# A two-layer decoder trunk on one core: weight buffers from a list, three lags, a third decay buffer and a new order of units in its DeltaNet layer

## The chip, the cores and the metric

The kernel runs on one core of one Trainium2 chip. The metric is the device time of the whole program in microseconds (us), the median of several runs. The core has five engines that run side by side, each through its own list of instructions in a fixed order: TensorE (PE in the profile; its weight loads are PEld), VectorE (DVE), ScalarE (ACT), GpSimd (POOL) and SyncE (SP), which issues most of the DMAs. An instruction that waits holds up all that stands behind it on its engine.

## The reference

528 positions (16 learned meta tokens and 512 of the input) of width 1024 pass two layers; each is a mixer (forgetting attention in layer 0, gated DeltaNet in layer 1) and a feed-forward block with a causal convolution, each with a norm before and after. The change lies in the DeltaNet layer:

```python
def gated_deltanet(h, w_in, conv_w, a_log, dt_bias, o_gain, w_out):   # H=8 heads of 128
    proj = hp @ w_in
    qkv, og, b_logit, a_logit = split(proj)
    qkv = silu(causal_dwconv(qkv, conv_w))
    q, k = l2norm(q) * Dh ** -0.5, l2norm(k)
    beta, g = sigmoid(b_logit), -exp(a_log) * softplus(a_logit + dt_bias)
    gc = cumsum(g)                                    # in each chunk
    dec = exp(where(incl, gc_i - gc_j, -inf))
    A = where(strict, kk * dec * beta, 0)
    sol = triangular_solve(A + I, [kc * beta * exp(gc), vc * beta])
    W, U0 = split(sol)
    def step(S, xs):                                  # one chunk after the other
        U = U0_n - W_n @ S
        O = qd_n @ S + qk_n @ U
        S = gl_n * S + U^T @ kd_n
        return S, O
    O = rmsnorm(O, o_gain) * silu(og)
    return O @ w_out
h = h + rmsnorm(m, g_post);  f = conv_ffn(rmsnorm(h, g_ffn));  h = h + rmsnorm(f, g_ffn_post)
```

All is float32. The kernel uses chunks of 16 and four times 128 positions.

## The kernel before

Every projection is cut into units of 128 output columns (`_units`, L68). A unit's weights come by one DMA into a staging tile (two of them), ACT casts them to a high part (L288) and DVE or POOL computes the low part (L295); `dense` (L303) then makes three matmuls for each of the (mostly 8) tiles of the inner dimension. The positions lie in two halves of 272 and 256. `push` (L428) runs the first half of a unit at once and the second half after a lag of further units: 4 with six weight buffers (`wp`), 6 between `wide` and `narrow` (L1477), where two more buffers (`wx`) exist. `need` (L298) loads one unit ahead. `boundary` (L405) is the norm between blocks: a sum of squares on ACT and POOL, a power on POOL, transposes on PE, then eight tiles of DVE work; the next projection needs its outputs `xh` and `xl`, and the scale `r` when a result leaves PSUM.

The DeltaNet layer (`deltanet` L844, `dn_heads` L902) has 33 input units: one for the gates, then K, V, Q and H (the output gate) for four groups of two heads, in the order of `DNSEQ` (L42). The gates become decays, which go to DRAM and come back broadcast. For each group there is a chain: `decays` (L1051) fills a decay buffer (two, taken in turn by the groups), `gram_k` (L1079) and `gram_q` (L1118) make the products K·K and Q·K, `solve_meta` (L1153) inverts the block of the meta tokens, `solve` (L1192) takes the 32x32 diagonal blocks through DRAM to POOL for a substitution of 31 steps (L1214, L1215), takes the result back and joins the blocks by four rounds of matmuls (m1 to m4), and `scan` (L1277) runs one meta step and four chunk steps. `heads_out` (L1364) normalises a chunk's output and transposes it into O. `part` (L866) multiplies the first four heads' O by the output weights (eight units P of four inner tiles); after the layer has been flushed, `out_proj` (L453) adds the other four heads' half (eight more such units), and `boundary` follows.

The order of PE's work in this layer is planned while the program is built. `Flow` (L219) keeps a clock of its own: each dense tile adds to it, and after each tile the tasks whose planned time has come put their instructions there. The distances between the steps of a task are the constants at the top (`T_HOP`, `T_GATES`, `T_OUT` and so on, in us). Dense matmuls and scan matmuls keep exactly the order in which they were written (`tok`, L267). PSUM has eight banks; in this layer dense results have two (`d`), grams two (`e`), scan steps two (`f`), scan outputs one (`g`), and the transposes of `heads_out` and all products of the solves share one (`h`).

The group chain waits on these flags before the change:

```python
yield lambda: ("gates", half) in done and (g < 2 or ("scan", g - 2) in done) and (half or not g or ("meta", g - 1) in done)
...
if g:
    yield lambda: ("sub", g - 1) in done
yield from solve()
```

Of the kernel before, what the change touches and what calls it, by code (L numbers as in the profile page):

```python
# [29 lines left out]
T_HOP = 1.4  # L30
T_CONV = 7
T_SUMS = 4
T_GATES = 13
T_BLOCKS = 8
T_DMA = 3.5
T_STEP = 1.0
T_META = 2.0
T_BACK = 6
T_INV = 3
T_OUT = 3.5  # L40

DNSEQ = [(x[0], int(x[1])) for x in "K0 V0 Q0 K1 K2 Q1 V1 H0 Q2 K3 V2 H1 Q3 V3 H2 H3 P0 P1 P2 P3".split()]  # L42
# [25 lines left out]
def _units():  # L68
# [26 lines left out]
    for kind, g in DNSEQ:  # L95
        for hl in range(NG):
            if kind == "P":
                add("dn_w_out", 0, 0, 4, (NG * g + hl) * 128, 128)
                continue
            add("dn_w_in", 0, 0, 8, {"Q": 0, "K": 1024, "V": 2048, "H": 3072}[kind] + (NG * g + hl) * 128, 128)  # L100
    for m in range(8):
        add("dn_w_out", 0, 512, 4, m * 128, 128)
# [5 lines left out]
def trunk(ctx, tc, h0, wflat, params, out):  # L108
# [10 lines left out]
    wp = ctx.enter_context(tc.tile_pool(name="wp", bufs=6))  # L119
# [11 lines left out]
        "dn": {"ps": "d", "g": "e", "s": "f", "o": "g", "t": "h", "l": "h"},  # L131
# [87 lines left out]
    class Flow:  # L219
# [38 lines left out]
        def until(self, cond):  # L258
            assert not self.busy
            while not cond():  # L260
                t = min(self.ready(), key=lambda t: t["wake"])
# [13 lines left out]
    state = {"next": 0, "lag": LAG}  # L275

    def load(u):
        _, _, _, nk, _, M = units[u]
        n = nk * M
        pool = wp  # L280
        if "wx" in state and units[u][0] != "dn_w_in" and u % 4 == 3:
            pool = state["wx"]
        wl = pool.tile([P, n], F32R, name="wl", tag="wl")
        wh = pool.tile([P, n], F32R, name="wh", tag="wh")
        w32 = ws.tile([P, n], F32, name="w32", tag="w32")[:]
        with tc.high_priority(offset=0):
            nc.sync.dma_start(w32, wflat[int(offs[u]):int(offs[u + 1])].rearrange("(p f) -> p f", p=P))
            nc.scalar.copy(wh[:], w32)  # L288
# [14 lines left out]
    def dense(u, half, xh, xl, c0=0, c1=None):  # L303
# [4 lines left out]
        o = ps[:M, 0:c1 - c0]  # L308
        tot = 3 * nk
        i = 0  # L310
        for k in range(nk):
            a = slice(k * M, (k + 1) * M)
# [114 lines left out]

    def push(u, fn):  # L428
        need(u)
        while len(pending) >= state["lag"]:  # L430
            a, f = pending.pop(0)
            f(a, 1)
# [3 lines left out]
    def flush():  # L436
        while pending:
            a, f = pending.pop(0)
            f(a, 1)
# [404 lines left out]
    def deltanet(layer, post, pre, wcx):  # L844
# [5 lines left out]
        m = [None, None]  # L850

        def split(half, k0):
            c = CUT if half == 0 else 0
            n = HALF[half][1] if n_cut else HALF[half][1] - c
            x = take(half, "ohl", F32R, [P, 2, KT // 2, n])
# [6 lines left out]
        n_cut = []  # L862
# [3 lines left out]
        def part(u, half, mt):  # L866
            n = HALF[half][1] - (CUT if half == 0 else 0)
            if mt == 0:
                drop(*X[half][:2])
                m[half] = take(half, "m", shape=[P, KT, n])  # L870
                OHL[half] = split(half, 0)
            x = OHL[half]
            ps = dense(u, half, lambda k: x[:, 0, k, :], lambda k: x[:, 1, k, :], 0, n)
# [668 lines left out]
```

## Time and profile before

| | us |
|---|---|
| median of 3 runs (lowest, highest) | 1616.88 (1613.69, 1617.59) |
| the profiled execution's own time | 1616.02 |
| its span in the profile | 1614.3 |
| PE busy in the span | 1521.4 (94%) |
| PEld, DVE, ACT, POOL busy | 1489.7, 1140.3, 801.9, 458.2 |

PE's busy time is an upper bound of useful work: matmuls overlap in the pipeline, and the time counts at whichever clock the throttle grants. So the count of matmuls in a stretch, the granted clock (1.00 is 2.4 GHz, 0.5 is 1.2 GHz) and the gaps are to be read together.

### The profile page before, as it was taken

The numbers are of one execution on the slowest core, as the hardware profiler recorded it, in microseconds if no ns is written. First come the engines' busy times: TensorE is split into PE (matmuls) and PEld (weight loads), VectorE is DVE, ScalarE is ACT, GpSimd is POOL, SyncE is SP. The second block draws the span as 40 slices with busy tenths as digits, with TensorE's granted clock in tenths as the row PEclk, the third lists the DMA queues.
The fourth block names the chain that finished last, engine by engine and source line by source line (L and its number), as shares of the span: only waits on it lengthen the run. The fifth ranks groups of instructions, "written<-read, shape, count | busy, mean of one in ns | idle before, by whom it ended". The sixth has DMA issues, their size and how long they took to land.

```text
span 1614.3 us, 32996 instructions
## 1 busy us (share of the span) xinstructions
PE 1521.4 (94%) x12462; PEld 1489.7 (92%) x12462; DVE 1140.3 (71%) x2765; ACT 801.9 (50%) x1868; POOL 458.2 (28%) x951
## 2 busy tenths in 40 slices
PE   8999999999999999999779889899989999999996
PEld 6999999899999999999678879889978999999996
DVE  7888888949974675665878757675559864765764
ACT  6677777735543442343454355444555543433441
POOL 6434443125200010013544562633044100100112
PEclk9999999999999999999799789999998999999998
DMA  5332222422223222322233322221241323323321
GB/s 173 90 88 77 74 87 74 133 68 77 93 82 102 92 82 90 95 89 82 81 90 93 92 62 61 75 69 37 80 137 54 93 90 93 99 85 97 99 68 53
DMA packets 67680, 139.56 MB, mean 86 GB/s; under 512 B 22936, under 2 KB 35640, under 8 KB 67136
## 3 DMA queue, kind: packets, MB, share of 16 engines
q1 hardware_dynamic: 66896, 135.08, 28.2%
q8 instruction: 98, 1.61, 0.4%
q0 software_dynamic: 480, 2.15, 0.4%
q14 instruction: 62, 0.51, 0.1%
q10 hardware_dynamic: 144, 0.22, 0.0%
HBM read 132.06 MB, written 5.36 MB: 85 GB/s over the span
## 4 chain that ended last, share of the span: by engine, by line
PE 68%; DVE 11%; POOL 6%; DMA 5%; ACT 4%; issue 3%; SPq 2%; POOLq 0%; DVEq 0%; ACTq 0%
PE ps L315 62%; POOL RB L1215 3%; POOL PR L1214 3%; DVE h L415 1%; DVE bt L414 1%; DVE wl L295 1%; DMA w<-wflat 1%; PE av L701 1%; DVE cv L767 1%; DVE xl L381 1%; DMA AB<-dA 1%; PE pt L681 1%; DMA gcr<-gcd 1%; ACT wh L288 1%; DVE qr L580 1%
## 5 line engine op out<-in xcount | busy, mean ns | idle before, releaser
L315 PE MATMUL ps<-xh,wh 128*128 128x256 f32 (+4 forms) x2464 | 720.6, 294 | 26.6 <-DVE ub L751 19.1
L315 PE MATMUL ps<-xl,wh 128*128 128x256 f32 (+4 forms) x2464 | 713.4, 290 | 6.1 <-DVE xl L381 6.0
L315 PE MATMUL ps<-xh,wl 128*128 128x256 f32 (+4 forms) x2464 | 716.3, 291 | 0.0
L315 PEld LDWEIGHTS ps<-xh,wh 128*128 128x128 f32 (+1 forms) x2464 | 473.9, 193 | 31.2 <-DVE ub L751 11.9
L315 PEld LDWEIGHTS ps<-xl,wh 128*128 128x128 f32 (+1 forms) x2464 | 474.3, 193 | 10.2 <-DVE xl L381 8.1
L315 PEld LDWEIGHTS ps<-xh,wl 128*128 128x128 f32 (+1 forms) x2464 | 474.1, 193 | 0.9 <-DVE wl L295 0.3
L288 ACT CAST wh<-w 128x1024 fp32r<-128x1024 f32 (+3 forms) x226 | 224.9, 996 | 194.2 <-PE ps L315 166.2
L295 DVE TENSOR_TENSOR wl<-w,wh 128x1024 fp32r<-128x1024 f32 (+4 forms) x191 | 221.0, 1157 | 100.7 <-ACT wh L288 100.0
L767 DVE SCALAR_TENSOR_TENSOR cv<-ub,prm,cv 128x256 f32<-128x256 f32 (+2 forms) x494 | 244.0, 499 | 37.5 <-ACT cv L758 29.4
L315 PE MATMUL ps<-ah,wl 128*128 128x256 f32 (+2 forms) x704 | 199.8, 284 | 0.0
L315 PE MATMUL ps<-ah,wh 128*128 128x256 f32 (+2 forms) x704 | 199.6, 284 | 0.0
L315 PE MATMUL ps<-al,wh 128*128 128x256 f32 (+2 forms) x704 | 199.4, 284 | 0.0
L758 ACT ACTIVATE cv<-ub,prm 128x256 f32<-128x256 f32 (+2 forms) x224 | 113.5, 510 | 142.3 <-DVE ub L751 142.0
L751 DVE TENSOR_TENSOR ub<-ps,r 128x256 f32<-128x256 f32 (+2 forms) x224 | 95.3, 427 | 95.5 <-PE ps L315 94.7
L315 PEld LDWEIGHTS ps<-ah,wh 128*128 128x128 f32 x704 | 132.9, 189 | 0.0
L315 PEld LDWEIGHTS ps<-al,wh 128*128 128x128 f32 x704 | 132.7, 189 | 0.0
L315 PEld LDWEIGHTS ps<-ah,wl 128*128 128x128 f32 x704 | 132.6, 189 | 0.0
L356 POOL TENSOR_TENSOR ssq<-ssq,sq 128x256 f32<-128x256 f32 (+2 forms) x98 | 90.1, 922 | 148.4 <-ACT sq L355 146.9
L754 POOL COPY cy<-ub 128x2 f32<-128x2 f32 (+1 forms) x112 | 35.5, 319 | 294.1 <-DVE ub L751 293.3
L295 POOL TENSOR_TENSOR wl<-w,wh 128x512 fp32r<-128x512 f32 x70 | 94.5, 1370 | 72.1 <-ACT wh L288 56.7
L750 POOL COPY ub<-cy 128x2 f32<-128x2 f32 (+1 forms) x112 | 30.0, 268 | 208.2 <-DVE cv L767 172.7
L814 DVE TENSOR_TENSOR m<-m,ps 128x256 f32<-128x256 f32 (+2 forms) x64 | 27.2, 425 | 42.6 <-PE ps L315 42.5
(340 smaller groups left out, 2442.7 us busy)
## 6 DMA issues: line engine op xcount, KB each, us to landing
w<-wflat SPq DMA_DIRECT2D x176, 512.0 KB, 3.6
w<-wflat SPq DMA_DIRECT2D x32, 448.0 KB, 3.2
cB<-cdram SPq DMA_DIRECT2D x16, 264.0 KB, 3.5
w<-wflat SPq DMA_DIRECT2D x16, 256.0 KB, 2.7
h<-h SPq DMA_DIRECT2D x8, 272.0 KB, 4.9
cB<-cdram SPq DMA_DIRECT2D x16, 136.0 KB, 3.0
h<-h SPq DMA_DIRECT2D x8, 256.0 KB, 5.5
AB<-dA SPq DMA_DIRECT2D x16, 128.0 KB, 3.7
```

The source lines that it names most:

```text
L288: nc.scalar.copy(wh[:], w32)
L295: eng.tensor_tensor(wl[:, c], w32[:, c], wh[:, c].bitcast(F32), op=ALU.subtract)
L315: tok(nc.tensor.matmul(o, w[:, a], r[:, c0:c1], start=(i == 0), stop=(i == tot - 1)))
L356: nc.gpsimd.tensor_tensor(self.acc[:, :n], self.acc[:, :n], sq[:, :n], op=ALU.add)
L750: nc.gpsimd.tensor_copy(ub[:, 0:c0], carry.pop(ft)[:, :c0])
L751: nc.vector.tensor_tensor(ub[:, c0:c0 + n], ps, r[:, :n], op=ALU.mult)
L754: nc.gpsimd.tensor_copy(c[:, :c0], ub[:, n:n + c0])
L758: nc.scalar.activation(cv, ub[:, c0:c0 + n], AF.Identity, scale=w[c0])
L767: nc.vector.scalar_tensor_tensor(cv, ub[:, i:i + n], w[i], cv, op0=ALU.mult, op1=ALU.add)
L814: nc.vector.tensor_tensor(mm, mm, ps, op=ALU.add)
L1214: nc.gpsimd.tensor_tensor(t, R3[:, 0:a, l:l + 1].to_broadcast([P, a, w]), A3[:, l:l + 1, l + 1:32].to_broadcast([P, a, w]), op=ALU.mult)
L1215: nc.gpsimd.tensor_tensor(R3[:, 0:a, l + 1:32], R3[:, 0:a, l + 1:32], t, op=ALU.subtract)
```

## The change

Weight buffers: `wh` and `wl` of a unit become one tile in a slot taken from a list `wfree` and given back when the unit's second half has been written; beside six `wp` slots the list holds two of the activation slots at the start of the DeltaNet layer, and the two `wx` slots in the feed-forward block. Lags: 6 up to the second unit of K1, then 3, and 4 from the point at which scan 2 has been planned. A third decay buffer, which takes one `wp` slot, serves group 2; group 3 takes that of group 0. The order of units changes (H1 earlier, Q2 and V2 later). The output projection has units of 256 columns and four inner tiles: four P for the first heads, four R for the others, all inside the layer's planned order; each half waits for its own outputs. `solve` writes its blocks to DRAM before it waits for the substitution ahead of it, and reads them after. Flags keep a planned distance between users of one PSUM bank (`take_g`, `take_l`). The planning constants get new values, and `heads_out` has two more planned distances. On ACT both VB go ahead of both KD. The constants and the order of units stand on joined lines below; the long DMA patterns are cut.

```diff
-T_HOP = 1.4 / T_CONV = 7 / T_SUMS = 4 / T_GATES = 13 / T_BLOCKS = 8 / T_DMA = 3.5 / T_STEP = 1.0 / T_INV = 3 / T_OUT = 3.5
+T_HOP = 1.6 / T_CONV = 8 / T_SUMS = 3 / T_GRAM = 4.5 / T_GATES = 15 / T_BLOCKS = 5 / T_LOAD = 5 / T_DMA = 4 / T_STEP = 1.02
+T_INV = 2 / T_R = 2.6 / T_U = 2.0 / T_S = 1.7 / T_OUT = 2.6 / T_POW = 2.4 / T_OT = 1.5 / T_BANK = 1.8
-DNSEQ: K0 V0 Q0 K1 K2 Q1 V1 H0 Q2 K3 V2 H1 Q3 V3 H2 H3 P0 P1 P2 P3
+DNSEQ: K0 V0 Q0 K1 K2 Q1 V1 H0 H1 K3 Q2 V2 H2 Q3 V3 H3 P0 P1 R0 R1
 def load(u):
-        pool = wp
-        if "wx" in state and units[u][0] != "dn_w_in" and u % 4 == 3:
-            pool = state["wx"]
-        wl = pool.tile([P, n], F32R, name="wl", tag="wl")
-        wh = pool.tile([P, n], F32R, name="wh", tag="wh")
+        i = next(i for i, x in enumerate(wfree) if x[0] != "wx" or units[u][0] != "dn_w_in")
+        kind, j = sl = wfree.pop(i)
+        if kind == "x":
+            w = take(j, "w", F32R, [P, 2, n])
+        else:
+            w = wpools[kind].tile([P, 2, n], F32R, name="w", tag=f"w{j}")
+        wslot[u] = sl, w
+        wh, wl = w[:, 0, :], w[:, 1, :]
...
 def part(u, half, j, last):
+            for sub in range(2):
+                mt = 2 * j + sub
+                ps = dense(u, half, lambda k: x[:, 0, k, :], lambda k: x[:, 1, k, :], 0, n, sub)
+                if not last:
+                    nc.vector.tensor_copy(mm, ps)
+                    continue
+                nc.vector.tensor_tensor(mm, mm, ps, op=ALU.add)
+                ssm[half].add(mm)
...
+            if j == 3:
+                drop(x)
+                if last:
+                    boundary(half, m[half], ssm[half], post, pre)
...
 def decays(half):
-                    if g % 2 not in Gs:
-                        Gs[g % 2] = take(g % 2, "ATQD", shape=[P, 2, 4 * NG, P])
+                    if g < 2:
+                        Gs[g] = take(1 - g, "ATQD", shape=[P, 2, 4 * NG, P])
+                    elif g == 2:
+                        Gs["w"] = wfree.pop(0)
+                        Gs[2] = wp.tile([P, 2, 4 * NG, P], F32, name="ATQD", tag=f"w{Gs['w'][1]}")
+                    G = Gs[g % 3]
...
 def solve():
+                for b in range(4):
+                    nc.sync.dma_start(dA[...], AT[bs, :, bs])
+                yield T_BLOCKS
+                if g:
+                    yield lambda: ("sub", g - 1) in done
                 AB = ...; RB = ...; memsets of RB
-                for b in range(4):
-                    nc.sync.dma_start(dA[...], AT[bs, :, bs])
                 for r in range(4):
                     nc.sync.dma_start(AB[32 * r:32 * r + 32, :], ...)
-                yield T_BLOCKS
+                yield T_LOAD
...
 def scan():
-                        nc.scalar.activation(KD[hl][:], p[:, 256:384], AF.Copy, scale=cc("kd", hl))
-                    yield T_HOP + 1.2
+                    for hl in range(NG):
+                        nc.scalar.activation(KD[hl][:], px[hl][:, 256:384], AF.Copy, scale=cc("kd", hl))
+                    yield T_R
...
 def heads_out(ci, po, MO):
                 nc.gpsimd.tensor_tensor(mo, mo, mhalf[:, 0:nh], op=ALU.pow)
+                yield T_POW
                 (OU on ACT and DVE)
-                yield 0.0
+                yield T_OT
+                yield take_l()
                 pt = psum_tile("t")
+                held["l"] = flow.now + T_BANK
...
 def kchain(half):
-                yield lambda: ("gates", half) in done and (g < 2 or ("scan", g - 2) in done) and (half or not g or ("meta", g - 1) in done)
+                yield lambda: ("gates", half) in done and (g < 3 or ("scan", 0) in done) and (half or not g or ("meta", g - 1) in done) and decayed[0] == 2 * g + half and (g != 2 or half or wfree)
...
+                if (kind, g, hl) == ("K", 1, 1):
+                    state["lag"] = 3
+                    while len(pending) > 3:
+                        second()
+                    wfree[:] = [x for x in wfree if x[0] != "x"]
+                if kind in "PR":
+                    state["lag"] = LAG if ("scan", 2) in done else 3
+                    def fp(u, half, j=NG * g + hl, last=kind == "R"):
+                        for x in range(8 // NG) if last else range(4 // NG):
+                            flow.until(lambda: ("out", x, half) in done)
+                        if last and half:
+                            flow.until(lambda: ("scan", 3) in done)
+                        part(u, half, j, last)
```

## Rows read from the trace of the kernel before

**Rows 1.** The page's header and its first part: busy time, share of the span and number of instructions of each engine.

```profile
span 1614.3 us, 32996 instructions
PE 1521.4 (94%) x12462; PEld 1489.7 (92%) x12462; DVE 1140.3 (71%) x2765; ACT 801.9 (50%) x1868; POOL 458.2 (28%) x951
```

**Rows 2.** Busy time of each engine by stage. Columns: the stretch, its length, then busy us and instructions of PE, PEld, DVE, ACT and POOL, the granted clock, the DMA share and GB/s. The first row is the feed-forward block of layer 0; the others cover the passage into the DeltaNet layer, the gates, the group chains, and the passage out of the layer.

```profile
340.00:755.00 415.00, 413.96 (x3369) 412.54 (x3370) 276.45 (x518) 175.16 (x328) 69.62 (x170) 1.00 0.28 90
755.00:800.00 45.00, 35.38 (x224) 32.26 (x224) 38.59 (x83) 21.39 (x48) 23.77 (x39) 0.77 0.28 96
800.00:835.00 35.00, 28.89 (x221) 28.45 (x220) 24.94 (x45) 22.94 (x45) 17.66 (x25) 0.90 0.22 62
835.00:1180.00 345.00, 311.40 (x2717) 301.83 (x2715) 237.57 (x747) 163.37 (x453) 138.27 (x374) 0.93 0.28 72
1180.00:1250.00 70.00, 58.39 (x422) 56.20 (x421) 54.80 (x109) 39.01 (x84) 36.01 (x50) 0.88 0.34 102
```

**Rows 3.** The waits of PE from 800 to 1180 us: who waited for whom, us in total, times, longest.

```profile
PE ps L315 <- DVE ub L751: 14.1, 5, 5.2
PE t L1378 <- ACT OU L1374: 7.7, 3, 4.5
PE s L1305 <- ACT KD L1302: 5.2, 4, 2.6
PE g L1042 <- DVE ATQD L1104: 2.2, 2, 1.7
PE s L1311 <- ACT U L1307: 1.9, 2, 1.5
PE t L1378 <- ACT ATQD L1272: 1.6, 2, 0.9
PE l L1264 <- POOL PR L1214: 1.5, 1, 1.5
...
```

**Rows 4.** Stretches of 10 us, in the columns of Rows 2.

```profile
770.00:780.00 10.00, 4.42 (x19) 2.16 (x19) 9.91 (x26) 3.82 (x10) 5.92 (x15) 0.64 0.25 81
...
810.00:820.00 10.00, 4.81 (x40) 4.60 (x38) 8.31 (x14) 6.75 (x10) 4.40 (x5) 0.86 0.17 50
960.00:970.00 10.00, 7.01 (x31) 5.96 (x32) 5.62 (x17) 5.60 (x21) 0.98 (x3) 0.66 0.41 93
1040.00:1050.00 10.00, 6.28 (x32) 6.29 (x33) 6.56 (x25) 3.52 (x7) 1.78 (x3) 0.66 0.47 121
1180.00:1190.00 10.00, 7.75 (x52) 7.37 (x51) 5.47 (x13) 4.26 (x12) 1.43 (x5) 0.83 0.53 163
```

**Rows 5.** The waits of PE from 1180 to 1250 us.

```profile
PE psn L345 <- POOL ssq L356: 4.2, 2, 2.8
PE psn L368 <- POOL nst L366: 3.1, 3, 1.5
PE t L1378 <- ACT OU L1374: 2.2, 1, 2.2
```

**Rows 6.** The chain of work that ended last, from 1178 to 1216 us: start, length, what.

```profile
1182.43 0.88 PE t L1378 x2
...
1184.44 2.70 DMA w<-wflat
...
1188.54 3.73 DMA w<-wflat
...
1196.49 5.38 DMA w<-wflat
...
1204.28 3.62 DMA w<-wflat
```

**Rows 7.** The same chain from 865 to 925 us, around the end of group 0's substitution and the start of group 1's.

```profile
909.70 1.97 DMA dR<-RB
...
917.07 1.68 DMA dA<-ATQD
...
920.18 4.29 DMA AB<-dA
```

**Rows 8.** Instructions of POOL in order of time during group 0's substitution (start, length, line, shape): its first step, two steps that took long with a neighbour each, and its last.

```profile
875.73 0.47 POOL L1214 TENSOR_TENSOR PR<-RB,AB 128x31 f32<-128x31 f32 x1 [1.11 <-DMA AB<-dA]
...
893.91 2.13 POOL L1214 TENSOR_TENSOR PR<-RB,AB 128x70 f32<-128x70 f32 x1
...
896.52 0.31 POOL L1214 TENSOR_TENSOR PR<-RB,AB 128x65 f32<-128x65 f32 x1
...
907.43 0.22 POOL L1215 TENSOR_TENSOR RB<-RB,PR 128x8 f32<-128x8 f32 x1
```

**Rows 9.** The costliest groups of POOL's instructions, first from 875 to 908 us (group 0), then from 1075 to 1103 us (group 3): count, busy us, mean ns, idle before.

```profile
L1215 POOL TENSOR_TENSOR RB<-RB,PR 128x60 f32<-128x60 f32 (+24 forms) x31 | 13.2, 426 | 2.2
L1214 POOL TENSOR_TENSOR PR<-RB,AB 128x60 f32<-128x60 f32 (+24 forms) x31 | 12.7, 408 | 2.8 <-DMA AB<-dA 1.1
...
L1215 POOL TENSOR_TENSOR RB<-RB,PR 128x60 f32<-128x60 f32 (+24 forms) x31 | 11.2, 360 | 2.3
L1214 POOL TENSOR_TENSOR PR<-RB,AB 128x60 f32<-128x60 f32 (+24 forms) x31 | 9.5, 307 | 2.8 <-DMA AB<-dA 0.7
```

**Rows 10.** Busy time of each engine during the same two substitutions, in the columns of Rows 2.

```profile
875.00:908.00 33.00, 29.53 (x220) 29.36 (x220) 25.76 (x87) 11.57 (x26) 28.38 (x76) 0.90 0.25 64
...
1075.00:1103.00 28.00, 24.95 (x232) 24.02 (x231) 12.59 (x37) 13.14 (x36) 22.14 (x67) 0.82 0.10 26
```

More of the change, by code (lines that the diff above doesn't have):

```diff
@@ L28 @@
 NF = 22
[L30 to L36, printed above, removed]
+T_HOP = 1.6
+T_CONV = 8
+T_SUMS = 3
+T_GRAM = 4.5
+T_GATES = 15
+T_BLOCKS = 5
+T_LOAD = 5
+T_DMA = 4
+T_STEP = 1.02
 T_META = 2.0
 T_BACK = 6
-T_INV = 3
-T_OUT = 3.5
-DNSEQ = [(x[0], int(x[1])) for x in "K0 V0 Q0 K1 K2 Q1 V1 H0 Q2 K3 V2 H1 Q3 V3 H2 H3 P0 P1 P2 P3".split()]
+T_INV = 2
+T_R = 2.6
+T_U = 2.0
+T_S = 1.7
+T_OUT = 2.6
+T_POW = 2.4
+T_OT = 1.5
+T_BANK = 1.8
+DNSEQ = [(x[0], int(x[1])) for x in "K0 V0 Q0 K1 K2 Q1 V1 H0 H1 K3 Q2 V2 H2 Q3 V3 H3 P0 P1 R0 R1".split()]
 NG = 2
@@ L260, in until @@
             while not cond():
+                if not self.ready():
+                    self.now += 0.5
+                    continue
                 t = min(self.ready(), key=lambda t: t["wake"])
@@ L275, in trunk @@
     state = {"next": 0, "lag": LAG}
+    wfree = [("wp", i) for i in range(6)]
+    wslot = {}
+    wpools = {"wp": wp}
     def load(u):
@@ L301, in need, with release, dense @@
             state["next"] += 1
-    def dense(u, half, xh, xl, c0=0, c1=None):
+    def release(u):
+        sl, w = wslot.pop(u)
+        if sl[0] == "x":
+            drop(w)
+            if state["lag"] < 6:
+                return
+        wfree.append(sl)
+    def dense(u, half, xh, xl, c0=0, c1=None, sub=None):
         wh, wl, nk, M = loaded[u]
@@ L426, in trunk, with second @@
     pending = []
+    def second():
+        a, f = pending.pop(0)
+        f(a, 1)
+        release(a)
     def push(u, fn):
@@ L850, in deltanet @@
         m = [None, None]
+        ssm = [None, None]
+        NT = (272 - CUT, 256)
         def split(half, k0):
             c = CUT if half == 0 else 0
-            n = HALF[half][1] if n_cut else HALF[half][1] - c
-            x = take(half, "ohl", F32R, [P, 2, KT // 2, n])
+            x = take(half, "ohl", F32R, [P, 2, KT // 2, NT[half]])
             o = O[half][:, :, c:]
@@ L897, in deltanet @@
         phase("ffn")
         wide(wcx)
-        out_proj(srcs, post, pre, reload, m, lambda half: drop(OHL[half]))
-        flush()
     def dn_heads(layer, O, cx, part):
@@ L981, in gates, with take_g, take_l @@
             flow.spawn(columns(), T_GATES)
+        held = {"g": False, "l": 0.0}
+        def take_g():
+            return lambda: not held["g"]
+        def take_l():
+            return lambda: held["l"] <= flow.now
         GT = {}
@@ L1121, in gram_q @@
                 w = len(CI[half])
-                sqs = squares(half, Q)
                 egs = []
@@ L1127, in gram_q @@
                     nc.sync.dma_start(egs[hl][:, :n], gcd[hd:hd + 1, s:s + n].to_broadcast([P, n]))
+                yield T_DMA - T_SUMS
+                sqs = squares(half, Q)
                 yield T_SUMS
+                yield take_g()
+                held["g"] = True
                 pn = psum_tile("g")
-                sums(half, sqs, pn)
+                yield from sums(half, sqs, pn)
                 pv = pn[:, 0:w * NG].rearrange("p (c x) -> p c x", x=NG)
```

170 lines of the change are left out of this document (99 added, 71 removed).

## The prediction

> **What bounds the kernel now.** I read the header first: PE is busy 94% of the span, DVE 71% [rows 1]. So only work that PE stands still for, or does at a lower clock, can be won. Then the busy time by stage: in the feed-forward block PE is busy for 413.96 of 415 us at full clock and issues 3369 matmuls, one per 0.123 us [rows 2]. Nothing that the change touches can be won there. From 755 to 1250 us, in the DeltaNet layer and its two passages, it is otherwise. Two losses are to be seen in each row. Idle time is the length less PE's busy time: 45 − 35.4 = 9.6 in the passage in, 35 − 28.9 = 6.1 at the gates, 345 − 311.4 = 33.6 in the chains, 70 − 58.4 = 11.6 in the passage out; 60.9 us in all. The second is the clock, (1 − granted clock) times the length: 0.23 × 45 = 10.4, 0.10 × 35 = 3.5, 0.07 × 345 = 24.2, 0.12 × 70 = 8.4; 46.5 us [rows 2]. They overlap a little, so about 100 of these 495 us could at most be won. The two belong together: the stretches with a clock of 0.64 to 0.86 are those in which PE stood for some us in the 10 us shown or just before [rows 4].
>
> Then the waits tell who ends the idle time in the chains: PSUM not yet emptied by DVE (14.1), the output tile OU not ready for its transposes (7.7), the scan's operands (5.2 and 1.9), and little else; PE waits for the substitution for 1.5 us in all [rows 3]. So the serial chain of the groups doesn't set the end: PE always has dense work to put beside it, and it loses its time in many short stops, because its fixed order puts some instruction a few us too early.
>
> **The change part by part.** All sums are against the profiled execution, 1616.0 us, of which 1614.3 is the span; that is 0.9 below the median of 1616.9.
>
> *heads_out.* Between the squares and the transposes the plan has 3.5 us now (T_OUT, then nothing) and 2.6 + 2.4 + 1.5 = 6.5 after. The waits for OU are 7.7 in three, with a longest of 4.5 [rows 3], and 2.2 at the end [rows 5]: 9.9 us in four. Three us later each, the longest leaves 1.5 and the others nothing: −8.4. The waits put down to ATQD at the same transposes, 1.6 [rows 3], are a collision in the shared bank, which the flag is for: −1 of 1.6 (from 0 to −1.6). The clock follows: the stretches at 960, 1040 and 1180 us have 0.66, 0.66 and 0.83 [rows 4], so they lose 3.4, 3.4 and 1.7. The first also has scan waits in it, so I credit two thirds of the 8.5: −5.7. Sum −15, bounds −20 and −6 (the first if the clock comes back whole, the second if only half of the waits go and no clock).
>
> *VB ahead of KD.* Four waits at L1305 of 5.2 us [rows 3] are put down to KD copies, which stand between the two heads' VB on ACT. Moving one copy out takes at most the whole wait and at least nothing: −5.2 to 0. The copies are short beside the 1.3 us of a mean wait; I take −1.5.
>
> *The passage out.* Now the second half of the projection comes after a flush: eight loads of 256 KB, each for 12 matmuls per half, and the chain shows four loads in a row, 2.70 + 3.73 + 5.38 + 3.62 = 15.4 us of the 26 from 1182.4 to 1208 [rows 6], while PE needs 24 × 0.123 = 3.0 us a unit. After, four units R of 512 KB have 48 matmuls each (5.9 us), and their first halves stand between the second halves of P, so the loads are covered; and half 0 need not wait for the last two chunks of scan 3. If that cover were gone, the chain of loads would return with its 15.4 us. What stays are the norm's own waits, 4.2 and 3.1 [rows 5], since `boundary` is not changed; the second halves behind it grow from 72 to 96 matmuls, +2.9 us of cover. The stage loses 11.6 + 8.4 = 20.0 [rows 2]; without OU's 2.2 and 1.7 that is 16.1; with 7.3 left and its clock I put 8: −8, bounds −14 and +3 (the norm of half 1 is then the longest).
>
> *Third decay buffer, and the blocks' DMA ahead of the wait.* Group 1's blocks went out at 917.1 and came back after 924.5, 12.8 us behind the end of group 0's results at 911.7 [rows 7]; of that some 5 us go. Group 2 need not wait for scan 0. Both shorten a chain for which PE waits 1.5 us [rows 3]: −0.5, bounds −1.5 and 0. Price: one weight slot less and lag 3. A load has the time of four unit halves, 4 × 24 × 0.123 = 11.8 us, at either lag, since the slots in use are the lag and two; 0.
>
> *Lag 6 at the start.* Gates' second half now follows six first halves instead of four: 2 × 24 × 0.123 = 5.9 us later for the whole chain. But PE stood here for DVE (busy 9.91 of 10 us from 770 [rows 4]) and for its two dense banks, not for the second half's input, and the wait at 810 us (idle 5.2, clock 0.86 [rows 4]) comes while DVE works on the gates. Bounds −8 (that wait and its clock) and +5.9; I take 0, as DVE's work there is the same. The drain at K1 runs three second halves in a row, each emptied by the same DVE and ACT steps as before; 0.
>
> *Slots, combined tiles, flags, memsets.* In the feed-forward block the depth stays eight, with the same owner eight units before; 0, bounds ±1. The scan's meta step has four DVE memsets for two; off the path. The other bank flags take −1.
>
> *New stops.* Every constant and the order of units move, so PE's order is another one. The trace of before cannot show where it will stop: bounds −15 (about half of what the chains still lose) and +30 (as much idle as now once more). I take +4, near the row for scan operands, 5.2.
>
> Sum: −15 − 1.5 − 8 − 0.5 − 1 + 4 = −22, that is 1594 against 1616.0 and 1595 against the median.
>
> A rule that speaks against it: the Trainium skill, SBUF — State Buffer, section Who interferes with whom, says that a DVE instruction with two inputs in SBUF and a GpSimd instruction that reads SBUF exclude each other. The trace bears it out: one substitution step takes 2.13 us and a like one 0.31 [rows 8].
>
> **The rivals.**
>
> *A. PE comes near its floor.* With the chains of groups 2 and 3 early, half of the whole loss goes: (60.9 + 46.5)/2 = 54 less the overlap, some 48 us: 1568. For it: PE lacks no dense work anywhere in the chains. Against it: 14.1 us of waits are DVE's [rows 3], and its work is the same.
>
> *B. The substitution is slowed.* With the third buffer group 2's decays and grams fall beside group 1's substitution. Group 0's, with DVE busy for 25.8 of 33 us, has 834 ns a step; group 3's, with 12.6 of 28, has 667 [rows 9, 10]. That is 31 × 0.167 = 5.2 us a group, 10.4 for two. If the chain decided the end, the gain would shrink to −12: 1605. Against it: the 1.5 us that PE waits for it [rows 3].
>
> *C. Slower: the plan runs ahead of the chip.* The place is the scan. Its matmuls keep their written order, and with the groups' chains earlier each of 16 chunk steps may stand before its operands. Price: 16 × (5.2/4 + 1.9/2) = 36 us [rows 3], against −22 + −4 of my sum: +10, 1627; with the clock at two thirds of the idle time more. It decides once the chip is later than the plan by over about 2 us at most steps. For it: the plan's clock doesn't know of the half-clock stretches, 24 us in the chains alone [rows 2]. Against it: with much the same scan distances (T_R, T_U) the scan waits are 7.1 us in all now [rows 3].
>
> *D. It moves the stops without removing them.* 1616.
>
> **How the numbers follow.** Forecast (1580 to 1611) 0.52; A (under 1580) 0.19; B 0.07; D 0.09; C 0.13. The likeliest gives 1595. A measurement of this kernel can tell 0.3%, 4.9 us, from no change. Faster: forecast, A and B, 0.78; same: D, 0.09; slower: C, 0.13. The range leaves out the lower half of A and the upper half of C: 1566 to 1622.
>
> **What would show it.** Right: the waits at the transposes of OU fall from 11.5 us to under 3; the chain of weight loads after the last scan is gone; from 755 to the steady feed-forward work PE's idle time falls by some 13 and the clock's loss by some 9; the feed-forward blocks keep 0.123 us a matmul. Substitutions 1 and 2 stand nearly end to end, and PE still doesn't wait for them. Wrong: if PE's waits at L1305 and L1311 (scan operands) exceed 15 us, C holds; if the idle time stays at 61 us under other names, D; if the wait for DVE at the start of the layer grows, the lag's term was wrong. I would be most wrong if the order of PE, which I have not seen, puts a chain step early again and again.

## The result, and the profile after

The changed kernel takes 1620.96 us (median of 13 runs, 1616.66 to 1625.35) and the kernel before, beside it, 1615.21 (13 runs): ratio 1.0037, 95% interval 1.0023 to 1.0051. It is slower by about 6 us; forecast were 1595 and a gain. The time lies inside the forecast's outer range, 1566 to 1622, but at the end that was left open for rival C. The profiled execution took 1624.94 us, 4.0 above its median, so its losses are shown a little too large.

The page's header of the changed kernel, beside [rows 1]:

```profile
span 1623.0 us, 32915 instructions
...
PE 1528.3 (94%) x12462; PEld 1491.8 (92%) x12462; DVE 1144.3 (71%) x2760; ACT 800.0 (49%) x1849; POOL 456.2 (28%) x949
```

Its busy time by stage, in the columns of [rows 2]:

```profile
340.00:755.00 415.00, 413.87 (x3382) 413.25 (x3381) 275.17 (x519) 174.88 (x326) 73.65 (x173) 1.00 0.28 89
755.00:800.00 45.00, 31.36 (x186) 27.51 (x185) 40.51 (x84) 22.96 (x49) 29.09 (x39) 0.73 0.32 109
800.00:835.00 35.00, 29.47 (x227) 29.18 (x226) 26.46 (x46) 22.94 (x41) 13.91 (x22) 0.90 0.21 63
835.00:1180.00 345.00, 305.75 (x2638) 294.45 (x2637) 233.21 (x733) 157.97 (x436) 134.30 (x372) 0.92 0.28 73
1180.00:1250.00 70.00, 59.06 (x430) 55.65 (x429) 51.34 (x94) 33.52 (x73) 29.40 (x40) 0.93 0.27 83
```

Length less PE's busy time gives the idle time: 13.6, 5.5, 39.2 and 10.9 us, 69.4 with the rounding, for 60.9 before. The loss by the clock, (1 − granted clock) times the length, is 12.2 + 3.5 + 27.6 + 4.9 = 48.1 for 46.4 (a step of 0.01 in the clock of the chains is 3.5 us). Only the passage out is better by more than 1 us (20.0 to 15.8 in both together). The feed-forward block is as full as it was.

PE's waits from 800 to 1180 us, beside [rows 3]:

```profile
PE ps L339 <- DVE ub L778: 18.4, 7, 5.5
PE s L1395 <- ACT KD L1392: 7.1, 7, 2.1
PE s L1401 <- ACT U L1397: 4.2, 2, 3.9
PE t L1476 <- ACT OU L1470: 4.0, 3, 2.3
PE l L1359 <- DVE o L1484: 2.5, 1, 2.5
PE l L1220 <- DVE Y L1245: 2.5, 1, 2.5
PE l L1317 <- DVE Rm L1265: 1.9, 1, 1.9
```

Here `ub` is a dense result that DVE takes out of PSUM, KD and U are operands of the scan that ACT writes, OU is the normalised output ahead of its transposes, `o` what DVE makes of those, and Y and Rm belong to the inverse of the meta block. The reader is to see what went and what came. The waits for OU fell from 7.7 to 4.0 (forecast were under 3 with those of the shared bank), and the 2.2 after 1180 us [rows 5] are gone. At the same time the waits for ub rose from 14.1 to 18.4, for KD from 5.2 to 7.1, for U from 1.9 to 4.2; `o` is new with 2.5, and Y and Rm have 2.5 and 1.9 for 1.7 and 0.7 before.

The chain that ended last, behind the last scan (start, length, what), beside [rows 6]:

```profile
1183.36 5.42 PE ps L339 x45
1188.78 0.22 PE t L1476 x2
1189.00 10.21 PE ps L339 x84
...
1203.85 0.71 DVE w L310
...
1207.70 1.70 DVE w L310
...
```

No load of a weight is on it any more; PE works through to the norm. This part of the forecast came true as a picture. But PE's waits from 1180 to 1250 us are 10.8 us in all, for 11.6 before: those for the norm's sums [rows 5] are nearly gone, and others of the norm stand in their place, for `xl` and `xh`:

```profile
PE ps L339 <- DVE xl L405: 6.2, 7, 1.8
PE ps L339 <- ACT xh L404: 2.8, 1, 2.8
```

### The profile page after: what moved, and what is told of

The parts are those of the page before. It is cut to its first block, busy times and chain, and to the rows that moved or that the text cites. A ratio compares the mean times of both kernels' runs of the same rounds, so it can differ in the third digit from the quotient of the medians.

```text
span 1623.0 us, 32915 instructions
## 1 busy us (share of the span) xinstructions
PE 1528.3 (94%) x12462; PEld 1491.8 (92%) x12462; DVE 1144.3 (71%) x2760; ACT 800.0 (49%) x1849; POOL 456.2 (28%) x949
## 4 chain that ended last, share of the span: by engine, by line
PE 74%; DVE 11%; POOL 5%; ACT 4%; DMA 3%; issue 3%; SPq 1%; POOLq 0%; DVEq 0%; ACTq 0%
PE ps L339 64%; POOL PR L1295 2%; POOL RB L1296 2%; DVE bt L438 1%; DVE w L310 1%; DVE h L439 1%; PE av L728 1%; DMA gcr<-gcd 1%; DVE cv L794 1%; PE pt L708 1%; DVE xl L405 1%; ACT w L303 1%; PE sc L676 1%; PE sc L677 1%; PE pt L696 1%
## 5 line engine op out<-in xcount | busy, mean ns | idle before, releaser
L339 PE MATMUL ps<-xh,w 128*128 128x256 f32 (+5 forms) x4928 | 974.6, 292 | 30.6 <-DVE ub L778 19.4
L339 PEld LDWEIGHTS ps<-xh,w 128*128 128x128 f32 (+2 forms) x4928 | 793.8, 192 | 37.7 <-DVE ub L778 21.6
L339 PE MATMUL ps<-xl,w 128*128 128x256 f32 (+5 forms) x2464 | 713.2, 290 | 10.8 <-DVE xl L405 10.8
L339 PEld LDWEIGHTS ps<-xl,w 128*128 128x128 f32 (+2 forms) x2464 | 473.9, 192 | 15.7 <-DVE xl L405 13.9
L303 ACT CAST w<-w 128x1024 fp32r<-128x1024 f32 (+2 forms) x218 | 223.3, 1025 | 158.9 <-PE ps L339 143.3
L310 DVE TENSOR_TENSOR w<-w,w 128x1024 fp32r<-128x1024 f32 (+3 forms) x183 | 221.6, 1211 | 112.1 <-ACT w L303 112.1
L339 PE MATMUL ps<-ah,w 128*128 128x256 f32 (+2 forms) x1408 | 265.0, 284 | 0.0
L339 PEld LDWEIGHTS ps<-ah,w 128*128 128x128 f32 x1408 | 221.5, 188 | 0.0
L339 PE MATMUL ps<-al,w 128*128 128x256 f32 (+2 forms) x704 | 199.1, 283 | 0.0
L339 PEld LDWEIGHTS ps<-al,w 128*128 128x128 f32 x704 | 132.5, 188 | 0.0
```

The source lines that it names most:

```text
L303: nc.scalar.copy(wh, w32)
L310: eng.tensor_tensor(wl[:, c], w32[:, c], wh[:, c].bitcast(F32), op=ALU.subtract)
L339: tok(nc.tensor.matmul(o, w[:, a], r[:, c0:c1], start=(i == 0), stop=(i == tot - 1)))
```

## The experiments

Each kernel differs from another by the few lines shown. Ratios are to the kernel before, which ran on the same chip beside it; 0.001 is 1.6 us, and a difference of two ratios is uncertain by some 0.0017, 2.7 us. Three theories stood at the start: L, the gates come two unit halves late and carry the whole chain with them; S, PE's order is cut into many short stops behind DVE and POOL; P, the new distances make the plan's scans later.

**Four parts undone in the changed kernel (1.0037).**

e1, the lag at the start:

```diff
-        state["lag"] = 6
+        state["lag"] = LAG          # 4
-            if state["lag"] < 6:             # when an early slot is no longer given back
+            if ucur["u"] - DN0 > 8:          # the same unit, without the lag
```

> The changed kernel with a lag of 4 instead of 6 at the start of the DeltaNet layer (all else as changed). Theory L (the gates come two unit halves late and carry the whole chain with them): the gates' first DVE step moves from 811 to about 805 us and the time falls by 4 to 6 us, to a ratio of 0.999 to 1.001 against the kernel before. Theory S (the loss is many short stops of PE behind DVE and POOL): the time moves by less than 2 us, ratio 1.003 to 1.005. Rival P (a later plan of the scans leaves PE without dense work beside scan 0): scan 0's first VB comes earlier by some 6 us and the time falls by about 3 us.

Measured: 1613.39 us, ratio 0.9987 [0.9976, 0.9997]; 8.1 us back. The trace shows where it comes from. DVE and POOL in order of time, first in the changed kernel, at the gates' second half:

```profile
810.72 0.41 DVE L972 TENSOR_TENSOR gt<-ps,r 40x256 f32<-40x256 f32 x1
811.16 1.46 DVE L976 TENSOR_SCALAR gt<-gt,prm 40x528 f32<-40x528 f32 x1
...
811.04 2.74 POOL L310 TENSOR_TENSOR w<-w,w 128x512 fp32r<-128x512 f32 x2
```

and in e1:

```profile
804.34 0.42 DVE L972 TENSOR_TENSOR gt<-ps,r 40x256 f32<-40x256 f32 x1
804.79 0.49 DVE L976 TENSOR_SCALAR gt<-gt,prm 40x528 f32<-40x528 f32 x1
...
805.97 2.54 POOL L310 TENSOR_TENSOR w<-w,w 128x512 fp32r<-128x512 f32 x2 [1.32 <-ACT w L303]
```

The gates' first step starts 6.4 us earlier with a lag of 4, close to the 5.9 of the prediction's upper bound, and the end of the last U, ACT's last operand of the last scan, moves from 1181.7 to 1173.4 us. The delay goes through to the end. That is L, with one thing not separated: the second halves of group 0's keys, behind the gates, also come two units later with a lag of 6.

e2, twelve distances of the plan as before the change:

```diff
-T_GATES = 15        +T_GATES = 13
-T_LOAD = 5          +T_LOAD = 3
-T_OUT, T_POW, T_OT = 2.6, 2.4, 1.5
+T_OUT, T_POW, T_OT = 3.5, 0, 0      (and seven more by 0.02 to 1)
```

> The changed kernel with the planning constants of before (T_HOP, T_CONV, T_SUMS, T_GATES, T_DMA, T_STEP, T_INV, T_S, T_OUT as before; T_BLOCKS + T_LOAD = 8; T_POW = T_OT = 0; the bank flags stay). Theory P (the new constants plan the scans too late): scan 0 starts some 6 us earlier and the time falls by 4 us or more, ratio below 1.000; but the waits for OU come back, 4.0 to some 9 us. Theory S: the waits for OU come back and nothing is won, ratio 1.004 to 1.009.

Measured: 1615.01 us, 0.9998 [0.9988, 1.0007]; 6.3 us back. The gates stay late (811.5), but the substitution of group 3 starts at 1037 us for 1057. That is P's gain. P also expected the waits for OU to come back, and they don't, although the distances in heads_out are the old ones: PE's waits at these transposes are 2.2 us, less than the changed kernel's 4.0.

```profile
PE t L1476 <- DVE OU L1469: 1.4, 2, 0.9
PE t L1476 <- ACT OU L1470: 0.8, 1, 0.8
```

e3, two decay buffers in place of three:

```diff
-    G = Gs[g % 3]
+    G = Gs[g % 2]          (and the weight slot lent to group 2)
```

> The changed kernel with two decay buffers taken in turn, as before. Theory S (group 2's decays and grams, early, make DVE wait for their broadcasts and for POOL's powers behind the substitution, and PE waits for DVE to empty PSUM): PE's waits for DVE between 835 and 1180 us fall from 12.9 by 4 us or more and the time falls by 4 to 8 us, ratio 0.999 to 1.001. Theory L and theory P: the chain of groups 2 and 3 becomes late again and the time stays or rises, ratio 1.003 to 1.010.

Measured: 1618.82 us, 1.0027 [1.0016, 1.0038]; 1.6 us, within the uncertainty, and not the 4 to 8 of theory S.

e4, the units in the old order:

```diff
-H0 H1 K3 Q2 V2 H2 Q3 V3 H3
+H0 Q2 K3 V2 H1 Q3 V3 H2 H3
```

> The changed kernel with the order of units of before (Q2 and V2 early, H1 late). Theory P: with H1 late there is less dense work ahead of the point at which K3 or Q2 need a head buffer that scan 0 frees, so PE's idle time beside scan 0 grows and the time rises by 5 us or more, ratio above 1.006. Theory S: the order hardly counts, within 3 us, ratio 1.002 to 1.006.

Measured: 1621.5 us, 1.0037 [1.0024, 1.005]; nothing, against P.

**Two together, and parts alone.** e5 is e1's and e2's edits in one kernel.

> The changed kernel with a lag of 4 at the start of the layer (run e1) and the old distances of the plan (run e2) together. Alone they were worth 1621.0 - 1613.4 = 7.6 us and 1621.0 - 1615.0 = 6.0 us. If the late gates (theory L) and the places of the chain's steps in PE's order (theory P) are two losses, the two add up: about 1607.5 us, ratio 0.995 to the kernel before. If both are the same few stops of PE, met in two ways (theory S), the second brings little: 1612 to 1613.5 us, ratio 0.998 to 0.999.

Measured: 1604.52 us, 0.994 [0.9925, 0.9956], faster than both kernels. The two add up: 8.1 + 6.3 = 14.4 us expected from the changed kernel's 1621.0, 15.7 measured. Its busy time by stage from 755 us on, and PE's waits from 800 to 1180 us:

```profile
755.00:800.00 45.00, 31.33 (x186) 27.57 (x185) 40.48 (x84) 22.85 (x49) 29.11 (x39) 0.73 0.33 110
800.00:835.00 35.00, 31.08 (x244) 30.81 (x243) 26.70 (x52) 25.20 (x52) 14.71 (x24) 0.95 0.31 97
835.00:1180.00 345.00, 312.37 (x2785) 302.64 (x2785) 241.50 (x751) 162.18 (x448) 139.97 (x382) 0.96 0.29 77
1180.00:1250.00 70.00, 57.96 (x444) 54.78 (x443) 60.10 (x117) 36.93 (x79) 27.13 (x47) 0.98 0.23 71
```

```profile
PE ps L339 <- DVE ub L778: 14.6, 5, 5.3
PE s L1395 <- ACT KD L1392: 3.9, 5, 1.4
PE s L1384 <- DVE S L1448: 3.5, 1, 3.5
...
PE t L1476 <- ACT OU L1470: 2.1, 3, 0.9
```

The idle time is 62.3 us, about that of before; the loss by the clock is 29.1 for 46.4. By these sums e5's gain from 755 us on comes from the clock, not from less standing; PE issues 2785 matmuls in the chains for 2717. Why the clock stays up more isn't shown: the stops are about as long as before (ub has five waits in both, the longest 5.3 us for 5.2), and e8 below has the same 0.96 in the chains and gains nothing.

e6 puts back lag, distances, buffers and order; slots, units P and R, the blocks' DMA ahead of the wait, VB ahead of KD, the early slots and the flags stay.

```diff
 e1's + e2's + e3's + e4's edits
```

> The changed kernel with all four put back: lag of 4, old distances, two decay buffers, old order of the key and value units. What stays of the change: weight slots from a list, the output projection in units P and R with its halves apart, the blocks' DMA ahead of the wait, VB ahead of KD, the bank flags. If my terms for these hold (passage out -8, VB -1.5, flags -1), 1605 us, ratio 0.9935. If the passage out gains only what the end shows in the changed kernel (about 5 us at the norm's start), 1610, ratio 0.9965. If the flags cost as many stops as they save (theory S), 1615. If the third buffer is worth something once the start is not late, this run is slower than run e5; I expect 0 to 2 us slower.

Measured: 1614.32 us, 1.0001 [0.9988, 1.0013]. These parts, which I had put at −8, −1.5 and −1, give nothing together. e6 also keeps smaller edits, as all kernels made from the changed one do: the plan's time from a key unit to its gram is 4.9 us shorter than before at the old distances (T_DMA is taken off T_CONV, and the flag stands for T_HOP), and the plan counts more PE time for the solves.

e7 is the kernel before with the list of weight slots alone:

```diff
-        wl = pool.tile(..., tag="wl"); wh = pool.tile(..., tag="wh")
+        kind, j = wfree.pop(i)
+        w = wpools[kind].tile([P, 2, n], F32R, name="w", tag=f"w{j}")
```

> The kernel before with one part of the change: each weight is one combined tile from a list of eight slots. I priced this at 0 us (bounds 1 either way): 1615.4, ratio 1.000. But the changed kernel is about 4 us ahead at the end of attention (the 2000th dense matmul at 374.5 us for 378.5). If the slots make that, and it isn't eaten later, 1611.5, ratio 0.9975; if it is eaten where the gates wait for DVE at the start of DeltaNet, 1615 with DeltaNet's first waits longer by as much.

Measured: 1613.29 us, 0.9995 [0.9985, 1.0005]. Its attention, and with it that of the changed kernel, is ahead: the first 340 us in its row,

```profile
0.00:340.00 340.00, 328.65 (x2595) 312.44 (x2596) 279.12 (x815) 243.19 (x657) 136.26 (x163) 0.99 0.30 96
```

against 2573 matmuls before. The gates' first step comes at 800.4 us for 804.3, but the last U ends at 1180.1 for 1178.0. The 4 us are there and are lost again in the chains.

e8 is the kernel before with the three distances of heads_out alone, the prediction's largest term:

```diff
-T_OUT = 3.5
+T_OUT, T_POW, T_OT = 2.6, 2.4, 1.5   (with a yield for each)
```

> The kernel before with one part of the change: the distances in heads_out (2.6 + 2.4 + 1.5 in place of 3.5). By my prediction's largest term -15 us (bounds -20 and -6): 1600 us, ratio 0.991. By theory S (a stop taken from one place comes back at another, as PE's order is made out of all the steps together) 1613 to 1617, ratio 0.999 to 1.001, with the waits for OU under 3 us and as much idle time under other names.

Measured: 1615.25 us, 1.0006 [0.9996, 1.0015]. PE's waits from 800 to 1180 us:

```profile
PE ps L317 <- DVE ub L753: 16.8, 6, 5.2
PE g L1044 <- DVE ATQD L1106: 3.8, 2, 3.3
...
PE t L1381 <- ACT OU L1377: 3.2, 2, 2.2
PE s L1297 <- DVE S L1316: 2.9, 1, 2.9
...
```

OU's waits fell from 7.7 to 3.2, 4.5 us. The waits for ub rose by 2.7 and for ATQD by 1.6, and one of 2.9 for S is new: 7.2 us. The idle time from 755 to 1250 us is 63.0 us for 60.9: the stops were moved, not taken away. The stage of the chains:

```profile
835.00:1180.00 345.00, 308.60 (x2721) 296.06 (x2719) 237.84 (x749) 160.96 (x456) 140.55 (x375) 0.96 0.28 72
```

Its clock is 0.96 for 0.93, some 10 us by the sum used above, and yet it holds 2721 matmuls for 2717 and the last U ends at 1177.5 us for 1178.0. So neither sum, idle time or clock, is by itself a measure of the time.

**Parts taken back from e5 (0.994).**

e9, without the two early weight slots:

```diff
-        wfree.extend([("x", 0), ("x", 1)])
```

> Run e5 without the two extra weight slots at the start of the layer (six slots, as before the change, at the same lag of 4). In all runs of the changed kernel so far PE is busy for 31 of the 45 us from 755 us on, for 35.4 before and 34.3 in run e7, while the splits of the weights loaded early stand on DVE and POOL beside the norm. If these splits hold up the norm and the gates, the stage gets about 3 to 4 us back and the end with it: 1601 us, ratio 0.9915. If the norm is late for its own steps alone, 1604.5, ratio 0.994; if the extra slots cover loads that now come late, 1607 or more.

Measured: 1614.24 us, 0.9998 [0.9987, 1.001]; 9.4 us slower than e5, against my expectation. By stage:

```profile
755.00:800.00 45.00, 34.68 (x217) 31.20 (x216) 38.93 (x85) 21.66 (x48) 25.01 (x38) 0.77 0.27 96
800.00:835.00 35.00, 28.99 (x220) 28.38 (x219) 25.07 (x45) 22.47 (x45) 18.43 (x25) 0.90 0.19 62
835.00:1180.00 345.00, 303.25 (x2717) 292.41 (x2717) 241.08 (x746) 162.48 (x448) 137.59 (x377) 0.97 0.29 76
...
```

The 3.4 us in the first row come back as expected. But the next row loses 2.1 and the third 9.1: the first substitution starts at 880 us for 872, and so on to the last U (1173.4 for 1163.9). What the early loads cover there is not shown.

e10, e5 with two decay buffers, and e11, e5 with the old order (edits as in e3 and e4):

> Run e5 with two decay buffers in place of three. Run e6, which lacks the third buffer and the new order of units, was 10 us slower than e5. If the third buffer is what those 10 us are (group 2's chain starts 45 us earlier with it), 1614 us, ratio 1.000. If it is only worth what run e3 showed, where it cost 2 us, 1602 to 1604.5, ratio 0.993.

> Run e5 with the old order of the key, value, query and gate units. If the new order carries the 10 us between e5 and e6 (with it the keys of group 3 and the gates of group 1 come at other places), 1614 us, ratio 1.000. If run e4 holds here too, where the order was worth nothing, 1604.5, ratio 0.994. Between these, if the third buffer and the order need each other.

Measured: e10 1612.49 us, 0.9988 [0.998, 0.9997], 7.8 us slower than e5; e11 1610.29 us, 0.9967 [0.9955, 0.9979], 4.4 slower. The same two edits had cost the changed kernel nothing (e3, e4).

e12, e5 with no bank flags:

```diff
-            return lambda: not held["g"]
+            return lambda: True
-            return lambda: held["l"] <= flow.now
+            return lambda: True
```

> Run e5 with the bank flags taken out of the plan: no step of a chain is put off because another has just used the bank. My term for them was -1 us, so 1605.5, ratio 0.9945. If the flags are the reason that PE's own order stops less (waits at banks named after ATQD, M, Y), 1609 or more, ratio 0.997. If they delay the chains more than they save, 1602 or less.

Measured: 1620.03 us, 1.0032 [1.002, 1.0044]; 14.9 us slower, the largest single value of the study. The stage of the chains, beside e5's third row:

```profile
835.00:1180.00 345.00, 307.52 (x2653) 297.17 (x2653) 234.44 (x731) 156.88 (x431) 134.25 (x371) 0.92 0.27 70
```

132 matmuls fewer in the same 345 us: 4.9 us more idle time and a clock of 0.92 for 0.96, another 13.8 us. PE's waits at the banks that the flags guard (the grams' and the shared one) are 12.9 us for 12.4 in e5's trace, so about the same; longer are those in the scan (KD 7.2 for 3.9, and one of 4.2 for VB). The run also has no T_HOP ahead of `gram_k`, which the flag had replaced.

**Is it only the plan's chance?** Each edit makes another order of PE. So four kernels moved one distance by 0.1 us, which has no cause of its own.

```diff
 e13: e5              -T_HOP = 1.4    +T_HOP = 1.5
 e14: e5              -T_BANK = 1.8   +T_BANK = 1.9
 e15: kernel before   -T_HOP = 1.4    +T_HOP = 1.5
 e16: changed kernel  -T_HOP = 1.6    +T_HOP = 1.5
```

> Run e5 with one distance of the plan moved by next to nothing: T_HOP 1.5 us in place of 1.4. No step's real duration changes. If each part tried so far has a loss of its own (theory C, causes), this moves the end by under 2 us: 1603 to 1607, ratio 0.9925 to 0.995. If every small edit makes another order of PE, and an order is good or bad by several us without a cause that can be named (theory R, a rugged plan), it moves by 4 us or more, most likely up, since e5 is the lowest of twelve: 1608 to 1616.

> Run e5 with T_BANK 1.9 in place of 1.8, the time for which the plan holds the chains' bank after a use. Theory C: 1603 to 1607. Theory R: 1608 to 1616. If the flags' 15 us (run e12) are a matter of the bank being held just long enough, it is not slower.

> The kernel before with T_HOP 1.5 in place of 1.4 and nothing else. Theory C: within 2 us of the kernel before, ratio 0.9988 to 1.0012. Theory R: 3 us or more off, in either direction.

> The changed kernel with T_HOP 1.5 in place of 1.6 and nothing else (1.4 is the value before). Theory C: within 2 us of the changed kernel, ratio 1.0025 to 1.005. Theory R: 4 us or more off, more likely down, as the changed kernel is among the slowest: 1610 to 1617.

Measured: e13 1606.24 us, 0.9936 [0.9924, 0.9948]; e14 1608.7, 0.9953 [0.9941, 0.9965]; e15 1618.46, 1.0021 [1.0011, 1.0032]; e16 1624.1, 1.0054 [1.0042, 1.0066]. From their parents by −0.6, +2.1, +3.4 and +2.7 us. Each of these is uncertain by some 2.7 us itself; e15 alone is clear of no change. So, as far as four nudges can tell, an order is worth some 3 us by chance. The 6 to 15 us of lag, distances, early slots, third buffer (in e5) and flags stand above that; e3, e4, e7 and e8 don't, and e11 hardly.

**Which distances.** e17 is e5 with the changed distances in heads_out, e18 with those at the chains' entry.

```diff
 e17: -T_OUT, T_POW, T_OT = 3.5, 0, 0        +... = 2.6, 2.4, 1.5
 e18: -T_CONV, T_SUMS, T_GATES, T_DMA = 7, 4, 13, 3.5   +... = 8, 3, 15, 4
```

> Run e5 with the changed kernel's distances in heads_out (2.6 + 2.4 + 1.5 in place of 3.5), all other distances old. The nudges gave 0 to 3.4 us for no cause, so only more counts. By my largest term -15: 1590. In run e5 the waits at the transposes of OU are 3.4 us in the chains, so at most some 3 of gain are left: 1601.5 to 1605, ratio 0.992 to 0.994. If these three distances are what the changed kernel's new distances cost (1613.4 in run e1, 1604.5 in e5), because the transposes and the output projection behind them come 3 us later per head, 1610 to 1613.

> Run e5 with the changed kernel's distances at the entry of the chains (T_CONV 8, T_SUMS 3, T_GATES 15, T_DMA 4 in place of 7, 4, 13, 3.5). If the cost of the new distances lies here (keys and gates are asked for later in the plan, and everything behind them), 1610 to 1613 us, ratio 0.997 to 0.9985, with the first substitution later by 1 to 2 us. If it lies in the substitution and the scan (T_STEP, T_LOAD, T_INV, T_S, T_HOP) or in heads_out, 1604 to 1606.

Measured: e17 1612.5 us, 0.9985 [0.9973, 0.9997], 7.3 slower than e5; e18 1613.64, 0.9993 [0.9982, 1.0004], 8.6 slower. Either group alone costs as much as all twelve (e1 against e5: 7.6), so the cost isn't a sum over the distances. In e18 the first substitution starts nearly as in e5 (872.6 for 872.0 us, not 1 to 2 later) and group 3's at 1045 for 1028. The row of e17's chains:

```profile
835.00:1180.00 345.00, 308.09 (x2709) 299.00 (x2708) 237.25 (x740) 159.91 (x440) 135.75 (x377) 0.94 0.27 71
```

In e17 group 3's substitution starts nearly as in e5 (1031 for 1028 us), and the loss comes after it: VB of group 2's first scan step at 1066 for 1055, of group 3's at 1131 for 1123.

**The traces side by side.** Times in us; "rest" is the span less the end of the last U; idle and clock are summed over the four stages from 755 to 1250 us as above.

| kernel | gates' first step | substitution of group 2, 3 | last U ends | rest | idle | clock |
|---|---|---|---|---|---|---|
| before | 804.3 | 1004, 1075 | 1178.0 | 436.3 | 60.9 | 46.4 |
| after | 811.2 | 970, 1057 | 1181.7 | 441.3 | 69.4 | 48.1 |
| e1 | 804.8 | 959, 1049 | 1173.4 | 439.8 | 68.1 | 34.7 |
| e2 | 811.5 | 967, 1037 | 1174.5 | 437.7 | 68.7 | 29.1 |
| e5 | 803.8 | 958, 1028 | 1163.9 | 437.2 | 62.3 | 29.1 |
| e10 | 806.0 | 1014, 1081 | 1176.9 | 434.4 | 68.6 | 36.3 |
| e12 | 803.8 | 960, 1040 | 1179.7 | 439.0 | 65.9 | 46.4 |
| e17 | 803.5 | 958, 1031 | 1170.5 | 440.1 | 66.6 | 38.1 |

Over all 20 traces the rest lies between 430.7 and 441.3 us and doesn't follow the last U, which goes from 1163.8 to 1182.6. The end of the last scan tells most of the time, to within the 10.6 us of the rest. It doesn't follow the substitutions: group 3's starts 18 us earlier in the changed kernel than before, and the last U ends 3.7 us later; in e10 it starts last of all here, and the last U ends 1.1 us earlier than before.

## Why the prediction was wrong

*The premise.* "The serial chain of the groups doesn't set the end" held for the waits and failed for a late start. PE waits for the substitution no longer at all in the list above, and yet 6.4 us at the gates become 8 at the last U. A late chain need not be seen as a wait of PE for the chain, because PE's order is written by a plan in which the chain is late too; it is seen in the last scan's end. Starting the gates earlier shifted that end in both pairs where the lag alone differed: by 8.3 us (e1) and by 10.6 (e5 against e2). It is no law: e7's 4 us at the gates went elsewhere, and an earlier substitution of group 3 didn't bring an earlier end. Which step holds the last scan is not shown.

*The lag, taken as 0: the first step that failed.* It costs 8.1 us (e1) or 9.4 (e5 against e2), beyond my upper bound of 5.9, in e1 by less than the uncertainty. The 5.9 were worked out rightly (6.4 measured); wrong was the choice of 0 "as DVE's work there is the same". DVE's work is the same, but starts later, and the chain starts with it. Of the rest, 1.0 us is the longer step at 811.16.

*heads_out, −15: the step that failed by most.* The distances alone take most of the waits away, and the time doesn't fall: nothing alone (e8, interval −0.6 to +2.4 us; a gain of some 3 us could hide in the plan's chance, not 15), and 7.3 us slower in e5 (e17). I counted a wait's length as gain; e8 shows the same time under ub, ATQD and S. That is rival D's mechanism. My clock term, two thirds of 8.5 us, failed too: in e8 the clock of the chains rose and no time came of it. Nor are the distances needed for the shorter waits: with the old ones OU has 2.2 us in e2 and 3.2 in e5, for 7.7 before; what took the rest away there is not shown.

*VB ahead of KD, −1.5.* The term priced an edit that changes nothing on ACT. I had the KD copies between the two heads' VB, as the kernel's text has them; the trace of before has both VB ahead of both KD in all 16 chunk steps already, and where a wait is put down to KD, the first matmul starts 0.05 us after its own head's KD copy ends (ACT's rows, then PE's):

```profile
967.49 0.36 ACT L1300 ACTIVATE VB<-s,rho 128x128 f32<-128x128 f32 x1
...
968.37 0.37 ACT L1300 ACTIVATE VB<-s,rho 128x128 f32<-128x128 f32 x1
968.62 0.38 ACT L1302 ACTIVATE KD<-s,kd 128x128 f32<-128x128 f32 x1
...
969.16 0.37 ACT L1302 ACTIVATE KD<-s,kd 128x128 f32<-128x128 f32 x1
...
969.05 0.49 PE L1305 MATMUL s<-VB,ATQD 128*128 128x128 f32 x2 [1.16 <-ACT KD L1302]
```

These waits are for that copy. They are 7.1 us in the changed kernel for 5.2.

*The passage out, −8.* The chain of loads is gone. The stage's loss falls by 4.2 us, 3.5 of it by the clock, but from the last U to the end it takes 441.3 us for 436.3, and e6, which keeps this part, VB, the flags and the slots, is at 1.0001. Shown is that what e6 keeps brings nothing together; what each part brings in it wasn't tried apart.

*The flags, −1.* In e5 they are worth 14.9 us, as much as the largest term of my sum. I had only counted the waits that bore the bank's name, and those are as long without the flags. By their text they keep chain steps from being ordered where their bank is still in use; how that comes to 14.9 us, or how much of it is the missing T_HOP, is not shown.

*The third buffer, −0.5.* Nothing in the changed kernel (e3), 7.8 us in e5 (e10), where group 2's substitution starts 56 us earlier. *The slots, 0:* −0.8 us (e7). *The early slots*, which I had not priced apart, are worth 9.4 in e5: PE is busy for 3.4 us less in the passage in with them, and e9 shows that they give more in the next stages.

*New stops, +4.* Too small: e18's distances alone cost 8.6 us in e5.

*The rivals.* A: e5 gains 9.7 us of the 48. B: group 1's substitution has 675 ns a step (359 + 316), as the two groups of POOL's rows from 926 to 955 us say, far from group 0's 834 [rows 9] and under the 722 (346 + 376) of group 1 before:

```profile
L1295 POOL TENSOR_TENSOR PR<-RB,AB 128x60 f32<-128x60 f32 (+24 forms) x31 | 11.1, 359 | 8.4 <-DMA AB<-dA 6.3
L1296 POOL TENSOR_TENSOR RB<-RB,PR 128x60 f32<-128x60 f32 (+24 forms) x31 | 9.8, 316 | 2.1
```

C: it alone has the sign right, and the time lies near its 1627, but not for its reason: the scan waits it named are 7.1 + 4.2 = 11.3 us, under its 15. D came nearest as a mechanism, with more idle time, not the same. Of my signs of being right, the chain of loads went and the feed-forward block stayed as it was; the idle time rose by 8.5 us where I had 13 less.

*What stays open.* The values don't add up. Taken back from e5, lag, distances, early slots, third buffer, order and flags cost 9.4, 7.6, 9.4, 7.8, 4.4 and 14.9 us, 53 in all, and e5 is 9.7 faster than the kernel before. Each of these edits but the order's throws away most of the gain, one more than all of it. That the parts need each other is shown; why, step by step in PE's order, is not. The remaining distances (in the substitution and the scan) and the parts kept in e6 were not tried apart. And e5 was picked as the lowest of 18, so with a spread of 3 us a little of its gain may be luck; its nudged copies (0.9936 and 0.9953) say that most is not.

## What to carry to other kernels

In a kernel whose order on the busiest engine is written by a plan, don't count a wait's length as the gain of removing it: look at when the last serial step ends, and price every edit by what it does to that. Read the order of instructions on an engine from the trace, not from the kernel's text, before pricing a change of it. Raising a prefetch or pipelining depth delays the second halves too; ask whose first step waits behind them. Nudge a constant that means nothing to learn the plan's own spread, before reading a part's value, and undo parts both from the changed kernel and from the best one, since they don't add.

## What the runs showed of the hardware

The gates' first step, one DVE instruction with one input in SBUF and a column of scalars (40x528), takes 1.46 us beside POOL's split of a weight and 0.49 when POOL starts that split after it, as the two fences at e1 show; in e5, e10, e11, e12 and e17 it is 0.49 and the split starts behind it, in e2 and e9 1.45, and before 1.48, with the split under way. The Trainium skill, SBUF — State Buffer, section Who interferes with whom, names `tensor_scalar` among the instructions that can take the port pair that DVE shares with GpSimd; the trace agrees, with 1.0 us for this one.

The third buffer puts group 2's decays beside group 1's entry into its substitution. Each decay needs a gate row that a small DMA brings, and there are two buffers for these rows, so a load follows the decay that frees its buffer. The chain of the changed kernel there:

```profile
904.31 2.90 DMA gcr<-gcd
...
907.88 3.03 DMA gcr<-gcd
...
911.51 3.21 DMA gcr<-gcd
...
```

Three loads of a gate row in sequence, 9.1 us of 10.4, one behind the other's decay; DVE stood idle for 2.7 us of it. I had not priced that queue with the buffer; what it costs in time is not shown (e3, without it, is within the uncertainty).
